# Key and value projections of a hybrid attention and DeltaNet layer, two blocks at a time by seven half products

## The chip, the core and the metric

The kernel runs on one core of a Trainium2 chip. The metric is the device time of one execution in microseconds; the median of three runs is shown, and the profile is of one further execution with its own time. TensorE (PE in the profile, its weight loads PEld) multiplies 128x128 weight tiles with streams of up to 512 columns into PSUM, which the kernel divides into six single banks of 512 float32 columns and one double one; VectorE (DVE), ScalarE (ACT) and GpSimd (POOL) work elementwise; SyncE (SP) issues the DMAs.

## The reference

A decoder layer on 512 tokens and 16 meta tokens ahead of them (528 in all), width 1024, eight heads in each of two branches that read the same normalised input:

```python
hn = rms_norm(h, norm_w)                      # 528 x 1024
proj = hn @ w_in                              # blocks aq ak av az dq dk dv dz db da ga gd
# attention: two softmax maps of 64 columns a head, p = p0 - lam * p1
o_a = rms_norm(diff_attention(aq, ak, av, lam), attn_norm_w) * 0.8
y_a = (o_a * silu(az)) @ w_branch_attn
# gated DeltaNet: causal convolution over 4 tokens and silu on dq, dk, dv; l2 norms;
# chunks of tokens: t_inv = inverse of (1 + strict lower part of beta * k k' * decay)
u, w = t_inv @ (v * beta), t_inv @ (k * beta * exp(gc))
v_new = u - w @ state;  o = q_dec @ state + a_intra @ v_new;  state = state * cd + k_dec' @ v_new
y_d = (rms_norm(o, dn_norm_w) * silu(dz)) @ w_branch_delta
merged = sigmoid(ga) * y_a + sigmoid(gd) * y_d
out = rms_norm(h + merged @ w_out, final_norm_w)[16:]
```

## The kernel before

**Products.** The normalised input stands transposed in SBUF as hn: eight blocks of 128 channels by 528 tokens, each as a high part (hnH, rounded to the engine's fast 32-bit type) and a low part (hnL, the rest). A weight block (128 output channels) is loaded as 128x1024 `raw`, and `split` makes a high part wh by a ScalarE cast and a low part wl by a VectorE subtraction. `product` then runs three passes (high by high, low by high, high by low: `PASSES`) over eight channel blocks: 24 matmuls of 512 columns for aq, az, dz, ga and gd, 48 matmuls of 272 and 256 columns for ak, av, dk and dv, 48 of 258 for dq. `dense` runs the blocks in the order of `dense_order`: four groups of two heads each, then gd; yd and ya (the two branch projections) and ga follow.

**The tail's seven products.** For yd and ya, `split_pair` and `pair_products` take two weight blocks at a time by a Winograd scheme: both blocks and the tokens are halved, and seven half products (`PRODUCTS`, p1 to p7) take the place of eight. Four weight tiles wa to wd are made of sums of weight halves, the input's sums (bt tiles) are made in `branch`, and the accumulator r is copied away between p1, p6 and p7 (`snap`) and added to others (`total`).

**Around the products.** dk, dv and dq go through `conv_silu` (ScalarE copies the PSUM banks into a row xp, then a scale, three VectorE steps, a tanh, and a product). `delta_pair` does the DeltaNet of two heads: key transposes and norms, k k' and k q' products, a mask E of decays, the 32x32 blocks sent through DRAM (scrm) into a layout in which VectorE solves them in 31 x 2 dependent steps (ts), back through DRAM (scrt, tds), the inverses TT, then four chunks of recurrent steps and the output into od. `attention` does one head into oa. The gates az and dz are written into oa and od first (`after_gate`), and od and oa of all eight heads (16 tiles of 256 KB) stay in SBUF until the tail.

**What sets the order.** Each piece is a generator that yields the engine, slot or event that it needs next. `Plan` runs them once ahead of time with a cost for each instruction (`Engine.time`), takes the task that can start first (ties by rank: splits 0, conv and gates 1, attention 2, dense 4) and so writes a fixed instruction order for each engine. Tiles with few copies are slots (`SLOTS`), PSUM banks are shared by kinds (`BANKS`: two each for pd, the dense products; pat; pdl). On the chip each engine runs its list in that order. SP issues all DMAs from one such list, weights ahead of use as the four raw tiles come free.

Of the kernel before, what the change touches and what calls it, by code (L numbers as in the profile page):

```python
# [24 lines left out]
H = 8  # L25
# [8 lines left out]
def dense_order():  # L34

    order = []
    for g in range(H // 2):
        for n in ("dk", "dv", "dq"):
            order += [(n, 2 * g), (n, 2 * g + 1)]
        order += [(n, 2 * g) for n in ("ak", "aq", "az", "av")]  # L40
        order += [("dz", 2 * g), ("dz", 2 * g + 1)]
        order += [(n, 2 * g + 1) for n in ("ak", "aq", "az", "av")]
    order += [("gd", c) for c in range(KB)]
    for p in range(KB // 2):
        order += [("yd", 2 * p), ("yd", 2 * p + 1), ("ga", p)]
    for p in range(KB // 2):
        order += [("ga", KB // 2 + p), ("ya", 2 * p), ("ya", 2 * p + 1)]
    return order
# [7 lines left out]

ORDER = dense_order()
PASSES = ((0, 0), (0, 1), (1, 0))


BANKS = dict(pd=2, pat=2, pdl=2)
# [6 lines left out]
SLOTS = dict(raw=4, w=2, wo=4, W=4, sn=5, st=1, tf=1, psc=1, xp=2, y=2, kT=2, qT=2, ktd=2, vr=2, E=2, eg=2, AT=2, MT=2, sc=2, km=1,  # L68
             ts=1, msub=1, TT=1, aq=2, ak=1, vT=1, vs=1, e=4, pT=2, pm=2, ao=1, th=8)
# [139 lines left out]
class Engine:  # L209
# [18 lines left out]
    def time(self, op, args, kw):  # L228
# [5 lines left out]
        if self.name == PE:  # L234
# [3 lines left out]
            if dt == F32:  # L238
                small = ins[0].shape[0] <= 64
                return 2 * max(2 * n / 2.4, 27 if small else 107)  # L240
            if dt == F32R:
                return n / 2.4 + 2.7 if n >= 256 else max(2 * n / 2.4, 107)
# [16 lines left out]
def hybrid_block(ctx: ExitStack, tc: tile.TileContext, x, meta, wblk, wbd, wout, pcol, prow, out):  # L259
    nc = tc.nc  # L260
    plan = Plan({**SLOTS, "wo": 0}, BANKS, ALL_BANKS)
# [43 lines left out]
    def tick(event, n):  # L305
        ticks[event] = ticks.get(event, 0) + 1
        if ticks[event] == n:
            done(event)

# [78 lines left out]
    def split(n, raw):  # L388

        yield ("w" if n < len(ORDER) or n - len(ORDER) in (4, 5) else "wo",)  # L390
        if n < len(ORDER) or n - len(ORDER) in (4, 5):
            wh, wl = (mk(wp, [P, D], F32R, t, SLOTS["w"]) for t in ("wh", "wl"))
        else:
            wo_slot[n] = plan.task.slot
# [7 lines left out]
        give("raw")  # L402
        done(f"w{n}")

    pairs, wos, wo_slot = {}, [], {}

    def split_pair(n, raws):

        (a1, a2), half = raws, (slice(0, D // 2), slice(D // 2, D))
        name = ORDER[n][0], ORDER[n][1] // 2  # L410
        pairs[name] = tiles = {}

        def parts_of(key, src, cols=slice(0, D)):
            yield ("W",)
            which = plan.task.slot
            wh, wl = Ws[which]
            yield ACT
            A.copy(out=wh[:, cols], in_=src)
# [3 lines left out]
            done(f"{key} {name}")  # L422

        yield "Ws"
        yield from parts_of("wa", a1)
        yield ("st",)
        st = mk(late["fp"], [P, D], F32, "st", 1)
        yield DVE
        V.tensor_tensor(out=st[:, half[0]], in0=a2[:, half[0]], in1=a2[:, half[1]], op=ALU.add)
        yield DVE  # L430
        V.tensor_tensor(out=st[:, half[1]], in0=st[:, half[0]], in1=a1[:, half[0]], op=ALU.subtract)
        yield from parts_of("wb", st)
        yield DVE
        V.tensor_tensor(out=a2[:, half[0]], in0=a1[:, half[0]], in1=a2[:, half[0]], op=ALU.subtract)
        yield from parts_of("wc", a2)
        give("raw")
        yield DVE
        V.tensor_tensor(out=a1[:, half[1]], in0=a1[:, half[1]], in1=st[:, half[1]], op=ALU.subtract)
        give("st")
        yield from parts_of("wd", a1[:, half[1]], half[0])  # L440
# [1531 lines left out]
```

## Time and profile before

| | us |
|---|---|
| median of three runs | 770.39 (769.94 to 771.57) |
| the profiled execution | 769.52 |
| its span in the trace | 767.8 |
| TensorE busy | 748.4 |
| VectorE busy | 551.3 |
| ScalarE busy | 477.6 |
| GpSimd busy | 73.1 |
| moved by DMA | 68.59 MB |

The trace names a line of code, but all instructions go through one helper (L224), so groups are told apart by their tiles: `bank<-hnH,wh` is a matmul of a weight tile wh with hnH into a PSUM bank, `wl<-raw,wh` the VectorE subtraction that makes a low part. A time with a count is that of the group. A matmul's duration overlaps with its neighbours', so the distance of starts tells what one costs.

### The profile page before, as it was taken

The numbers are of one execution on the slowest core, as the hardware profiler recorded it, in microseconds if no ns is written. First come the engines' busy times: TensorE is split into PE (matmuls) and PEld (weight loads), VectorE is DVE, ScalarE is ACT, GpSimd is POOL, SyncE is SP. The second block draws the span as 40 slices with busy tenths as digits, with TensorE's granted clock in tenths as the row PEclk, the third lists the DMA queues.
The fourth block names the chain that finished last, engine by engine and source line by source line (L and its number), as shares of the span: only waits on it lengthen the run. The fifth ranks groups of instructions, "written<-read, shape, count | busy, mean of one in ns | idle before, by whom it ended". The sixth has DMA issues, their size and how long they took to land.

```text
span 767.8 us, 14456 instructions
## 1 busy us (share of the span) xinstructions
PE 748.4 (97%) x5479; PEld 687.6 (90%) x5479; DVE 551.3 (72%) x1287; ACT 477.6 (62%) x1288; POOL 73.1 (10%) x101
## 2 busy tenths in 40 slices
PE   5999999999999999999999999999999999999996
PEld 4999887999989899988899998879888998899785
DVE  6778695577778668669757776964687868789553
ACT  5378478588556779756677865466775436455232
POOL 3121012011001212101201200000100000000001
PEclk9999999999999999999999999999999999999999
DMA  8142423011342201234311123231123323233702
GB/s 306 32 124 82 136 63 94 29 56 56 96 126 90 64 29 56 83 91 131 70 57 56 56 87 99 85 78 55 29 83 111 111 79 109 87 111 91 266 1 110
DMA packets 41974, 68.59 MB, mean 89 GB/s; under 512 B 20344, under 2 KB 25252, under 8 KB 41904
## 3 DMA queue, kind: packets, MB, share of 16 engines
q1 hardware_dynamic: 41904, 67.66, 28.1%
q8 instruction: 43, 0.70, 0.4%
q14 instruction: 27, 0.22, 0.1%
HBM read 64.44 MB, written 3.21 MB: 88 GB/s over the span
## 4 chain that ended last, share of the span: by engine, by line
PE 87%; DMA 4%; DVE 4%; ACT 3%; issue 1%; SPq 1%; POOL 0%; POOLq 0%; ACTq 0%; DVEq 0%
PE bank L224 84%; PE psc L224 3%; DMA scrt<-ts 1%; DMA tds<-scrt 1%; DMA xt<-in_x_dram 1%; DVE wl L224 1%; SPq L224 1%; DMA raw<-in_wout_dram 1%; ACT ak L224 1%; DVE xr L224 0%; ACT wh L224 0%; DVE hnL L224 0%; ACT TT L224 0%; DVE th L224 0%; DVE Wl L224 0%
## 5 line engine op out<-in xcount | busy, mean ns | idle before, releaser
L224 PE MATMUL bank<-hnH,wh 128*128 128x512 f32 (+3 forms) x944 | 317.1, 338 | 0.8 <-ACT hnH L224 0.8
L224 PE MATMUL bank<-hnH,wl 128*128 128x512 f32 (+3 forms) x944 | 301.4, 321 | 0.0
L224 PE MATMUL bank<-hnL,wh 128*128 128x512 f32 (+3 forms) x944 | 301.2, 321 | 0.0
L224 PEld LDWEIGHTS bank<-hnH,wh 128*128 128x128 f32 x944 | 177.1, 189 | 14.2 <-ACT hnH L224 1.0
L224 PEld LDWEIGHTS bank<-hnH,wl 128*128 128x128 f32 x944 | 176.9, 188 | 13.9
L224 PEld LDWEIGHTS bank<-hnL,wh 128*128 128x128 f32 x944 | 177.4, 189 | 10.3
L224 DVE TENSOR_TENSOR wl<-raw,wh 128x1024 fp32r<-128x1024 f32 x82 | 100.7, 1228 | 40.7 <-ACT wh L224 40.2
L224 ACT CAST wh<-raw 128x1024 fp32r<-128x1024 f32 x82 | 85.9, 1048 | 37.3 <-PE bank L224 32.5
L224 DVE SCALAR_TENSOR_TENSOR y<-xp,pc,y 128x528 f32<-128x528 f32 (+1 forms) x72 | 54.7, 760 | 2.2 <-ACT y L224 1.3
L224 ACT ACTIVATE e<-psc,ast 128x144 f32<-128x144 f32 (+3 forms) x64 | 34.6, 542 | 10.9 <-DVE ast L224 10.6
L224 PE MATMUL bank<-btH,Wh 128*128 128x256 f32 x128 | 36.0, 281 | 1.4 <-ACT sn L224 1.4
L224 PE MATMUL bank<-btH,Wl 128*128 128x256 f32 x128 | 35.7, 279 | 0.0
L224 PE MATMUL bank<-btL,Wh 128*128 128x256 f32 x128 | 35.7, 279 | 0.0
L224 ACT CAST Wh<-raw 128x1024 fp32r<-128x1024 f32 (+1 forms) x24 | 21.6, 906 | 19.8 <-PE bank L224 12.6
L224 DVE TENSOR_TENSOR ts<-ts,tmps 99x84 f32<-99x84 f32 (+23 forms) x124 | 28.2, 228 | 2.5
L224 DVE TENSOR_TENSOR tmps<-msub,ts 99x84 f32<-99x84 f32 (+23 forms) x124 | 27.7, 224 | 2.5
L224 ACT ACTIVATE sqk<-bank 128x128 f32<-128x128 f32 x64 | 17.9, 279 | 18.4 <-PE bank L224 17.6
L224 DVE TENSOR_REDUCE ast<-psc 128x1 f32<-128x528 f32 (+3 forms) x40 | 28.6, 714 | 0.5
L224 PE MATMUL psc<-ak,aq 128*128 128x264 f32 (+3 forms) x160 | 28.9, 302 | 0.0
L224 DVE TENSOR_TENSOR Wl<-raw,Wh 128x1024 fp32r<-128x1024 f32 (+1 forms) x24 | 24.9, 1043 | 4.9 <-ACT Wh L224 4.9
L224 PEld LDWEIGHTS bank<-btH,Wh 128*128 128x128 f32 x128 | 24.0, 187 | 2.2 <-ACT sn L224 1.9
L224 PEld LDWEIGHTS psc<-ak,aq 128*128 128x128 f32 x160 | 23.9, 189 | 1.5
(336 smaller groups left out, 1506.5 us busy)
## 6 DMA issues: line engine op xcount, KB each, us to landing
raw<-in_wblk_dram SPq DMA_DIRECT2D x96, 512.0 KB, 3.5
raw<-in_wout_dram SPq DMA_DIRECT2D x8, 512.0 KB, 3.9
xt<-in_x_dram SPq DMA_DIRECT2D x4, 512.0 KB, 7.6
E<-gcd SPq DMA_DIRECT2D x8, 256.0 KB, 5.2
xr<-in_x_dram SPq DMA_DIRECT2D x8, 256.0 KB, 7.0
out_dram<-xr SPq DMA_DIRECT2D x8, 256.0 KB, 2.3
msub<-scrm SPq DMA_DIRECT2D x12, 128.0 KB, 2.6
scrt<-ts SPq DMA_DIRECT2D x4, 136.1 KB
```

What stands on the lines that cost most here:

```text
L224: return real(*args, **kw)
```

## The change

Fourteen pairs of blocks go by the seven half products: (dk 2g, dk 2g+1) and (dv 2g, dv 2g+1) of the last three groups, and (ak h, av h) of all eight heads. The tokens are halved at 264. For that the kernel keeps the whole transposed input as well (`whole_`, in tiles `room`), makes four sums of it once (`ts_h`, `ts_l`), and makes the four weight sums of each pair. The pair's results are put together in xp or vT: three ScalarE copies and four VectorE sums out of PSUM. A fourth accumulator q takes p4.

To have room for this in SBUF, od and oa keep two heads each (`RING`, in room 0 and 2); the output of heads 0 to 5 of both goes to DRAM and comes back when the token sums are done with. The gate of head h waits until head h-2 is out. E, eg, TT and other tiles of a head pair share one buffer TM, and the solve's msub lies in room 1.

`products` of the DeltaNet now makes only k k' and no longer waits for the queries; k q' is made in `queries`. The order in a group is keys, values, ak av aq az of the even head (in the first group after the queries), queries, dz, ak av aq az of the odd head, dz. ga comes one place earlier. Weight tiles are one set of three for all blocks, and six in the tail. The costs in `Engine.time` for matmuls are raised.

```diff
-        order += [(n, 2 * g) for n in ("ak", "aq", "az", "av")]
...
+        k, v, q, z = ([(n, 2 * g), (n, 2 * g + 1)] for n in ("dk", "dv", "dq", "dz"))
+        a0, a1 = ([(n, 2 * g + i) for n in ("ak", "av", "aq", "az")] for i in range(2))
+        order += k + v + (a0 + q + z[:1] if g else q + z[:1] + a0) + a1 + z[1:]
+    order += [("gd", c) for c in range(KB)] + [("ga", 0)]
...
+PAIR_PRODUCTS = {**PRODUCTS, "p4": ("q", "wc", 1, "t4")}
+LAST = ("p2", "p5", "p4", "p3")
...
-BANKS = dict(pd=2, pat=2, pdl=2)
+BANKS = dict(pd=3, pat=2, pdl=2)
...
-SLOTS = dict(raw=4, w=2, wo=4, W=4, sn=5, st=1, tf=1, psc=1, xp=2, y=2, kT=2, qT=2, ktd=2, vr=2, E=2, eg=2, AT=2, MT=2, sc=2, km=1,
-             ts=1, msub=1, TT=1, aq=2, ak=1, vT=1, vs=1, e=4, pT=2, pm=2, ao=1, th=8)
+SLOTS = dict(raw=4, W=3, st=1, cn=1, wo=4, sn=5, tf=1, psc=1, xp=3, y=2, kT=2, qT=2, ktd=2, vr=2, TM=1, AT=2, MT=2, sc=2, km=1,
+             ts=1, aq=1, ak=1, vT=2, vs=1, e=4, pT=2, pm=2, ao=1, th=2)
+RING = dict(od=2, oa=2)
...
-                return n / 2.4 + 2.7 if n >= 256 else max(2 * n / 2.4, 107)
+                return n / 2.4 + (11 if n < 400 else 18) if n >= 256 else max(2 * n / 2.4, 107)
...
+        def sums():
+            yield ("st",)
+            yield DVE
+            V.tensor_tensor(out=st[:, h0], in0=a2[:, h0], in1=a2[:, h1], op=ALU.add)
+            yield DVE
+            V.tensor_tensor(out=st[:, h1], in0=st[:, h0], in1=a1[:, h0], op=ALU.subtract)
+            done(f"wb sum {name}")
+            yield DVE
+            V.tensor_tensor(out=a2[:, h0], in0=a1[:, h0], in1=a2[:, h0], op=ALU.subtract)
...
+        for key, src, cols in (("wa", a1, both), ("wb", st, both), ("wc", a2, both), ("wd", a1[:, h1], h0)):
+            if key != "wa":
+                yield f"{key} sum {name}"
+            yield ("W",)
+            which = plan.task.slot
+            yield ACT
+            A.copy(out=Ws[which][0][:, cols], in_=src)
+            spawn(low(key, src, cols, which))
...
+            def whole():
...
+                            A.copy(out=whole_[2 * (c // 4) + m][:, :, lo - HALF * m:hi - HALF * m],
+                                   in_=pt[:, c - dst[1].start:c - dst[1].start + 4, lo - t0:hi - t0])
+                if tick(bank_, 2):
+                    give("pat", pt)
...
+        for key, (x_, y_) in dict(t1=(1, 0), t3=(3, 1), t2=(3, 0), t4=(2, 3)).items():
+            yield DVE
+            V.tensor_tensor(out=whole_[of_sum[key]], in0=whole_[x_], in1=whole_[y_], op=ALU.subtract)
+            spawn(high_low(key))
...
+    def spill(t, h):
+        yield SP
+        S.dma_start(out=out_of[t, h], in_=gate[t][h])
...
         A.activation(out=th, in_=pd, func=AF.Tanh, scale=0.5)
+        if h >= RING[t]:
+            yield f"{t} out {h - RING[t]}"
+        yield DVE
+        V.scalar_tensor_tensor(out=gate[t][h], in0=th, scalar=1.0, in1=pd, op0=ALU.add, op1=ALU.mult)
...
+    def queries(i):
+        h = hs[i]
+        yield f"dq{h}"
+        yield f"m{h}"
...
+    def pair_of_blocks(n):
...
+        def total(m, tau, of, key, src=None):
+            yield f"{key} {n}"
+            yield from take(m)
+            yield DVE
+            dst = to[m][:, tokens[tau]]
+            V.tensor_tensor(out=dst, in0=acc[of], in1=dst if src is None else src, op=ALU.add)
...
+            if key == "p4":
+                spawn(total(1, 1, "t", "c", cn), -1)
+            if key == "p3":
+                yield f"c+ {n}"
...
+                for m, (a, b) in enumerate(PASSES):
+                    T.matmul(acc[bk], w[a][:, k * P:(k + 1) * P], x_[b], start=fresh and k == 0 and m == 0,
+                             stop=k == KB // 2 - 1 and m == 2, skip_group_check=not fresh)
...
+        for n in range(3):
+            Ws.append([mk(gp, [P, D], F32R, f"w{t}{len(Ws)}") for t in ("h", "l")])
+            plan.give("W", len(Ws) - 1)
```

## Rows read from the trace of the kernel before

**Rows 1.** The page: busy time of each engine, and the chain by engine.
```profile
PE 748.4 (97%) x5479; PEld 687.6 (90%) x5479; DVE 551.3 (72%) x1287; ACT 477.6 (62%) x1288; POOL 73.1 (10%) x101
...
PE 87%; DMA 4%; DVE 4%; ACT 3%; issue 1%; SPq 1%; POOL 0%; POOLq 0%; ACTq 0%; DVEq 0%
```

**Rows 2.** Busy time by stage: the start, then the four head pairs.
```profile
core 0: us, PE busy (x) PEld busy (x) DVE busy (x) ACT busy (x) POOL busy (x), PEclk, DMA share, GB/s
0.00:20.00 20.00, 10.71 (x65) 9.84 (x66) 12.58 (x29) 11.15 (x21) 7.55 (x19) 1.00 0.83 305
20.00:152.00 132.00, 130.70 (x1027) 120.81 (x1028) 95.58 (x266) 86.32 (x241) 17.03 (x23) 1.00 0.27 80
152.00:281.00 129.00, 128.96 (x1019) 120.60 (x1018) 93.18 (x237) 90.74 (x272) 15.70 (x20) 1.00 0.26 77
281.00:411.00 130.00, 130.00 (x1029) 121.73 (x1029) 94.50 (x239) 91.87 (x278) 16.45 (x20) 1.00 0.26 76
411.00:541.00 130.00, 129.32 (x1003) 119.87 (x1002) 92.12 (x235) 85.84 (x260) 9.96 (x13) 1.00 0.23 72
```

**Rows 3.** TensorE in order: start, duration; first and last of two runs.
```profile
164.27 0.29 PE L224 MATMUL bank<-hnH,wh 128*128 128x272 f32 x1
...
165.66 0.29 PE L224 MATMUL bank<-hnH,wl 128*128 128x272 f32 x1
...
167.73 0.28 PE L224 MATMUL bank<-hnH,wh 128*128 128x256 f32 x1
...
170.06 0.28 PE L224 MATMUL bank<-hnH,wl 128*128 128x256 f32 x1
```

**Rows 4.** VectorE groups by shape: count, busy us, mean ns, idle before.
```profile
L224 DVE TENSOR_TENSOR wl<-raw,wh 128x1024 fp32r<-128x1024 f32 x82 | 100.7, 1228 | 40.7 <-ACT wh L224 40.2
L224 DVE SCALAR_TENSOR_TENSOR y<-xp,pc,y 128x528 f32<-128x528 f32 x48 | 36.7, 765 | 1.3 <-ACT y L224 0.6
...
L224 DVE TENSOR_TENSOR sn<-bank,sn 128x256 f32<-128x256 f32 x24 | 10.0, 421 | 9.9 <-PE bank L224 8.9 <-ACT sn L224 0.9
...
L224 DVE SCALAR_TENSOR_TENSOR kT<-xp,y 128x528 f32<-128x528 f32 x8 | 5.6, 698 | 0.0
```

**Rows 5.** VectorE in order, in the tail: start, duration.
```profile
600.71 0.42 DVE L224 TENSOR_TENSOR sn<-bank,sn 128x256 f32<-128x256 f32 x1
601.04 0.68 DVE L224 TENSOR_TENSOR raw<-raw,raw 128x512 f32<-128x512 f32 x1
...
699.74 1.22 DVE L224 TENSOR_TENSOR Wl<-st,Wh 128x1024 fp32r<-128x1024 f32 x1
700.88 0.68 DVE L224 TENSOR_TENSOR od<-th,oa 128x512 fp32r<-128x512 f32 x1
701.48 0.69 DVE L224 TENSOR_TENSOR raw<-raw,raw 128x512 f32<-128x512 f32 x1
702.08 0.42 DVE L224 TENSOR_TENSOR sn<-bank,sn 128x256 f32<-128x256 f32 x1
```

**Rows 6.** Busy time in stretches of 20 us, columns as in rows 2.
```profile
160.00:180.00 20.00, 20.00 (x169) 19.77 (x169) 18.54 (x48) 17.10 (x63) 3.80 (x6) 1.00 0.24 80
...
640.00:660.00 20.00, 20.00 (x91) 16.36 (x90) 19.02 (x30) 10.97 (x15) 0.00 (x0) 1.00 0.33 106
...
680.00:700.00 20.00, 20.00 (x158) 19.15 (x157) 19.27 (x33) 10.92 (x17) 0.00 (x0) 1.00 0.38 117
700.00:720.00 20.00, 18.55 (x134) 17.28 (x133) 18.43 (x29) 11.00 (x17) 0.00 (x0) 1.00 0.59 187
```

**Rows 7.** ScalarE groups by shape, columns as in rows 4.
```profile
L224 ACT CAST wh<-raw 128x1024 fp32r<-128x1024 f32 x82 | 85.9, 1048 | 37.3 <-PE bank L224 32.5 <-DMA raw<-in_wout_dram 2.9 <-PE psc L224 0.8
...
L224 ACT COPY sn<-bank 128x256 f32<-128x256 f32 x24 | 8.9, 372 | 22.2 <-PE bank L224 22.1
...
L224 ACT CAST hnH<-bank 128x512 fp32r<-128x512 f32 x8 | 4.7, 588 | 3.4 <-PE bank L224 3.4
```

**Rows 8.** The tile od on VectorE: ns least, median, most; first to last start.
```profile
L224 DVE SCALAR_TENSOR_TENSOR od<-bank,wD,od x8: 746/751/752, 159.4 to 558.4; 128x512 f32<-128x512 f32 x8
```

**Rows 9.** DMA issues: size, median us to landing.
```profile
out_dram<-xr SPq DMA_DIRECT2D x8, 256.0 KB, 2.3
```

**Rows 10.** The chain in order of time: start, us, what.
```profile
708.27 4.14 DMA raw<-in_wout_dram
```

## What the change was predicted to do

> **What bounds the kernel now.** I read the page's busy shares and its chain first, then a table by stage, then single matmul starts. TensorE is busy for 97% of the span and carries 87% of the chain that ended last [rows 1]. The stage table cuts the span at the four head pairs (20 to 541 us): TensorE is busy for 130.70 of 132, 128.96 of 129, 130.00 of 130 and 129.32 of 130 us there, at granted clock 1.00, its upper level (2.4 GHz) [rows 2]. A busy TensorE need not be a full one, so the starts decide: in one key block twelve 272-column matmuls start within 1.39 us (11 steps of 0.1264 us), and twenty-one 256-column ones within 2.33 us (20 steps of 0.1165 us) [rows 3]. Nothing fits between them. The kernel is bound by matmul columns, and every matmul that goes is worth its step as long as its neighbours still arrive on time.
>
> VectorE is the one to watch. In the same four stages it is busy for 95.58, 93.18, 94.50 and 92.12 us, together 375.4 of 521 us (72%); ScalarE has 354.8 [rows 2].
>
> **The matmuls removed.** Two blocks cost 48 matmuls of 272 and 48 of 256 columns now: 48 x (0.1264 + 0.1165) = 11.66 us. The seven half products are 7 x 4 x 3 = 84 matmuls of 264 columns; a step of 264 lies between the two rows, 0.1215 us, so 10.20 us. One pair saves 1.46 us, fourteen save **20.4 us** [rows 3]. All of it lies on TensorE's path. No other matmul count changes: the query products are only parted from the key products, and the seven-product tail stays.
>
> The rows show a fixed part of some 10 to 13 ns per matmul beside its columns at 2.4 GHz. The Trainium skill, TensorE: Matmul & The Clock Gate, section Back-to-back issue gap, gives columns/2.4 plus 2.5 ns for a lone stream; by it 264 columns take 112.5 ns and the saving is 18.9 us. The trace does not agree, its steps are longer; the row is taken.
>
> **What VectorE gets.** Back to back, a 1024-column subtraction holds VectorE for 1.14 us and a 512-column one for 0.60; a 256-column sum out of PSUM holds it for 0.33 [rows 5] (their listed durations, 1.228 and 0.421 us, overlap the next start [rows 4]). Per pair: low halves 3 x 1.14 + 0.60 against 2 x 1.14 now, +1.74; four sums of weight halves, +2.40; four sums of 264 columns from PSUM where ScalarE copied before, 4 x 0.34 = +1.36. Together **5.5 us**, 77 us for fourteen. The four token sums add four subtractions and four low halves of 1056 columns, 8 x 1.17 = 9.4 us (1.14 scaled to the columns). VectorE's load in the four stages rises from 375.4 to 461.8 us, while TensorE's floor there falls from 521 to 500.6: a share of 92%. That is the crux. Three 20 us stretches already stand at 18.54, 19.02 and 19.27 us of VectorE with TensorE at 20.00 of 20 [rows 6]: such a share is possible without a hole in TensorE, but it is shown for 20 us, not for 500.
>
> **Holes that this opens.** First, inside a pair: the last product may start only when the partial sum of r has been copied (0.372 us [rows 7]) and added into the block (0.421 [rows 4]) after the matmul's own 0.28 [rows 3]; the product between covers 12 x 0.1215 = 1.46 us. Slack is some 0.4 to 0.5 us. If VectorE has just begun a 1.14 us operation, TensorE waits up to 0.64 us; averaged over where in it the sum arrives, 0.64 x 0.64 / 2 / 1.14 = 0.18. Fourteen pairs: 0 to 9 us, I take 2.5. Second, three weight tiles turn over: a freed tile needs one cast (1.048 [rows 7]), one subtraction (1.14) and hops, some 2.7 us, and the tightest is needed 36 matmuls = 4.4 us later. Queueing of more than 1.7 us stops TensorE; one operation ahead on each engine makes 2.2, so 0 to 0.5 us at two tiles a pair, 0 to 14 us, I take 1.5 since both queues must be unlucky at once. Third, the key and value pairs stand back to back: with their convolutions (three steps and a product, durations in [rows 4], some 2.7 us a block) they ask 2 x 13.1 = 26.2 us of VectorE for 20.4 us of matmuls. Splits, sums and the one convolution that frees the third xp row come to 18.3, so the rest can lag into the query and gate products, where a block asks VectorE for under 4 us per 5.6. 0 to 5.8 us in each of three groups, I take 1 each: 3.
>
> **What is moved, at nothing.** The inverses start without the queries, so the 62-step solve runs under keys, values and attention products; the single shared buffer TM keeps the next head pair's decays behind this pair's last step, and its end leaves some 10 us before they are needed. The gate products wait for the spill of the head two before: head 0's output is written at 159.4 us [rows 8], and in the new order its successor's gate comes some 50 us of matmuls behind the group's start at 152; a 256 KB write lands in 2.3 us [rows 9]. If that cover went, a gate would hold one of three PSUM banks and VectorE's queue behind its multiply. On SP a spill that waits holds the weight loads behind it; four raw tiles are two pairs, 20 us, of cover. The way back begins after the last value pair, with eight gate blocks (over 40 us of matmuls) ahead of its first reader. One tile for scaled queries instead of two: the next head's comes 31 us of matmuls or more later.
>
> **Start and end.** Twelve copies of the transposed input into whole_ lengthen the hold on two PSUM banks in the first 30 us; ScalarE is busy for only 11.15 of the first 20 us [rows 2]. 0 to 1.2 us (two copies of 0.588 [rows 7] on the way), I take 0.5. At the end the gate blocks (ga) come one place earlier, so the output weights may come earlier than now, where a 4.14 us load stands in the chain [rows 10] and TensorE lacks 1.45 of 20 us [rows 6]; against that a merged block now waits for its neighbour. Between -1.4 and +1.4, I take 0.
>
> **Sum.** Profiled execution 769.52 (span 767.8 and 1.7 around it) - 20.4 + 2.5 + 1.5 + 3 + 0.5 = 756.6. The median of the three runs is 0.9 above the profiled one: **757.5 us**, 1.7% less.
>
> **Rivals.** (a) VectorE becomes the bound of the four stages. Their length is then 461.8 us over the share s that it sustains. At 0.90 that is 513, 8 less than now: 763 us; at 0.89, 769. For it: the load above, and one solve of 62 dependent steps per group during which other work must wait its turn. Against it: rows 6, and attention's backlog that VectorE can always draw on. The Trainium skill, Perfetto Trace Analysis, section Identifying the Most-Contended Engine, would judge VectorE by occupancy and TensorE by its weight loads, not by matmul busy time. By that rule VectorE, at 92%, would bound the stages ahead of TensorE's weight loads (90% of the span [rows 1]), which is this rival; the starts in rows 3 speak against it for the kernel before. (b) Slower: the same mechanism below its point of balance, 461.8 / 521 = 0.886. At s = 0.86 the stages take 537 us, 16 more: 787 us. The kernel before never needed more than 0.73 in any of the four [rows 2], so no row excludes it. (c) Each pair loses in its own chain what it saves, both upper ends above together (0.64 + 1.0 us of 1.46): 770 us, no change. (d) All covers hold and TensorE stays full: 770.4 - 20.4 = 750 us.
>
> **Chances.** Forecast (751 to 762) 0.58, (d) 0.08, (a) 0.14, (c) 0.06, (b) 0.14. Range 750 to 771: it leaves out most of (b) and the outer edge of (d). A measurement of this kernel tells 0.2%, 1.5 us, from no change. Faster: 0.58 + 0.08 + 0.14 = 0.80; same 0.06; slower 0.14.
>
> **What will show it.** TensorE should lose 168 matmuls and start its 264-column ones about 0.1215 us apart. If the forecast holds, its idle time in the four stages is 4 to 10 us, in pieces under 1 us that end on a sum (VectorE) or a low half, and the stages last some 508 us with VectorE at 0.90 to 0.92. If (a) or (b), the pieces are longer, end on VectorE throughout, and lie in the key and value pairs; if (c), they recur in every pair at the same product. The tail from the first branch product should last as before within 2 us. The prediction is wrong if VectorE's own load is more than 5.5 us a pair, if a gate waits for a spill, or if the way back from DRAM is late for the branch products.

## The result, and the profile after

The changed kernel takes 763.90 us in the median of fifteen executions (760.91 to 768.06), the kernel before 770.54: a ratio of 0.9906, 95% interval 0.9886 to 0.9925. That is 6.6 us less; 13 were forecast. The range of 750 to 771 holds it, the forecast's own 751 to 762 does not. One further execution of the changed kernel (3139 us) and one of the run e6_before_new_costs (2616 us) were slow as a whole and are not counted. The profiled execution is one of the longer ones, 767.75 us with a span of 766.0; a second profiled execution (762.45 us, span 760.7, the run a1_again) stands beside it below.

The page after, busy time of each engine and the chain by engine, answers [rows 1]:

```profile
PE 740.0 (97%) x5311; PEld 671.6 (88%) x5311; DVE 620.2 (81%) x1427; ACT 500.4 (65%) x1318; POOL 89.6 (12%) x102
...
PE 74%; DVE 10%; ACT 10%; issue 2%; DMA 1%; POOL 1%; SPq 0%; POOLq 0%; DVEq 0%; ACTq 0%
```

TensorE has exactly 168 matmuls less (5479 to 5311), but it carries 74% of the chain where it carried 87%: VectorE and ScalarE now stand in it with 10% each. Being "97% busy" before and after hides this. The stages, cut as in [rows 2]:

```profile
core 0: us, PE busy (x) PEld busy (x) DVE busy (x) ACT busy (x) POOL busy (x), PEclk, DMA share, GB/s
0.00:20.00 20.00, 8.69 (x50) 8.03 (x51) 12.89 (x26) 13.56 (x27) 8.71 (x20) 1.00 0.80 308
20.00:152.00 132.00, 128.72 (x991) 117.19 (x990) 114.76 (x294) 87.55 (x222) 25.01 (x21) 1.00 0.25 75
152.00:281.00 129.00, 127.37 (x957) 116.93 (x957) 110.30 (x273) 92.68 (x274) 15.83 (x20) 0.96 0.27 85
281.00:411.00 130.00, 129.32 (x1016) 119.80 (x1015) 113.29 (x280) 99.49 (x293) 19.49 (x20) 1.00 0.27 84
411.00:541.00 130.00, 129.32 (x983) 117.67 (x982) 108.08 (x276) 97.34 (x291) 14.05 (x15) 1.00 0.33 105
```

VectorE has 446.4 of 521 us (86%), 71.0 more than before; TensorE stands for 6.3 us in the four stages, where it stood for 2.0; and in the second stage the granted clock is 0.96, where it was 1.00 throughout. TensorE within one half product (start, duration; the first and the ninth of nine):

```profile
427.11 0.28 PE L231 MATMUL bank<-sumH,wh 128*128 128x264 f32 x1
...
428.08 0.28 PE L231 MATMUL bank<-sumH,wl 128*128 128x264 f32 x1
```

Eight steps take 0.97 us, 0.1213 each, against 0.1215 priced. The Trainium skill, TensorE: Matmul & The Clock Gate, section Back-to-back issue gap, has columns/2.4 plus 2.5 ns for an isolated matmul, by which it would be 112.5 ns; this trace does not agree with it, 264 columns at 2.4 GHz and 11 ns more fit.

What TensorE waited for (total us, times, longest; the first nine of fourteen rows):

```profile
PE bank L231 <- ACT st L231: 7.5, 1, 7.5
PE bank L231 <- ACT sn L231: 2.1, 1, 2.1
PE bank L231 <- DVE ss L231: 1.5, 1, 1.5
PE bank L231 <- DVE qT L231: 1.3, 3, 0.9
PE bank L231 <- DVE TM L231: 1.3, 3, 0.5
PE bank L231 <- ACT hnH L231: 1.3, 1, 1.3
PE bank L231 <- ACT pmT L231: 1.2, 1, 1.2
PE bank L231 <- ACT room L231: 0.9, 1, 0.9
PE bank L231 <- DVE sumL L231: 0.4, 1, 0.4
```

The first, third and sixth are the start; before, the same view has 7.3, 1.2 and 0.8 us for them. `pmT` (attention) and `sn` (the tail) have grown from 0.7 and 1.4 us. New are `room` (the second copy of the input holds a PSUM bank at the start) and `qT`, the scaled queries of the DeltaNet. `TM` stands where the kernel before had `td` and `t`, 1.2 us together. No wait ends on a weight tile (wh, wl), and none on a spilled gate. The longest wait for `qT` ends at 79.87 us. VectorE's list ahead of it (start, duration):

```profile
77.75 1.20 DVE L231 TENSOR_TENSOR wl<-raw,wh 128x1024 fp32r<-128x1024 f32 x1
78.88 0.33 DVE L231 SCALAR_TENSOR_TENSOR MT<-bank,sc,TM 128x128 f32<-128x128 f32 x1
79.15 0.67 DVE L231 SCALAR_TENSOR_TENSOR qT<-xp,y 128x512 f32<-128x512 f32 x1
```

So the short step stands behind a low half and a step of the DeltaNet, in a stretch in which VectorE has no room left. VectorE's 86% is an average of unequal stretches of 20 us, two of which are (columns as in the stages above):

```profile
60.00:80.00 20.00, 18.45 (x129) 16.27 (x128) 19.90 (x32) 16.72 (x40) 6.56 (x6) 1.00 0.03 5
300.00:320.00 20.00, 20.00 (x164) 19.56 (x163) 19.96 (x43) 19.50 (x59) 7.33 (x8) 1.00 0.47 156
```

VectorE is full in both. TensorE loses 1.55 us in the first, which has the waits for `qT`, and nothing in the second.

**The clock.** TensorE around 266 us, in the profiled execution; in brackets the idle time before, and what ended it:

```profile
265.55 0.28 PE L231 MATMUL bank<-hnH,wl 128*128 128x264 f32 x1
266.99 0.33 PE L231 MATMUL bank<-vm,pmT 96*128 96x128 f32 x1 [1.16 <-ACT pmT L231]
...
268.01 0.41 PE L231 MATMUL bank<-hnL,wh 128*128 128x264 f32 x1
268.22 0.42 PE L231 MATMUL bank<-hnH,wl 128*128 128x264 f32 x1
```

After 64 products of 32x32 (264.2 to 265.2), three matmuls and 1.16 us of waiting, the step of a 264-column matmul is 0.21 us instead of 0.12: the granted clock has fallen to its lower level, 1.2 GHz, and it stays there for 10 us. These 20 us in this execution (columns as in the stages above):

```profile
260.00:280.00 20.00, 18.84 (x159) 16.88 (x159) 11.20 (x23) 10.84 (x27) 0.27 (x1) 0.74 0.15 54
```

and in the second one, a1_again:

```profile
260.00:280.00 20.00, 18.81 (x198) 17.32 (x197) 12.72 (x28) 15.07 (x42) 1.01 (x1) 1.00 0.16 54
```

Clock 0.74 against 1.00, with the same instructions in the same order and the same wait ahead (1.16 us in both). In the profiled execution the clock falls once more, behind the tail's wait described below (0.91 over 700 to 720 us). So the clock falls in some executions and not in others, and the executions differ by it: at a mean clock of 0.996 to 0.998 they take 760.9 to 762.6 us, at 0.989 to 0.992 765.2 to 768.1. The kernel before takes 768.4 to 773.5 us in its executions, with medians between 769.4 and 770.9, and it too is slower where the mean clock is lower (769.4 at 0.998, 773.1 at 0.991).

**The tail.** The chain near 705 us (start, us, what), answering [rows 10]:

```profile
703.99 4.93 DMA raw<-in_wout_dram
708.92 0.02 issue
708.95 1.04 ACT wh L231
709.99 0.28 ACT sn L231
710.27 0.04 issue
710.32 1.80 PE bank L231 x12
```

ScalarE's list has the cast of the fifth output weight block ahead of the copy `sn` of a partial sum. The block's load is late, the cast waits for it, the copy waits behind the cast, and TensorE waits 2.1 us (3.0 in the second execution) for a copy of 0.28 us that had nothing to do with the load.

### The profile page after: what moved, and what is told of

Same layout as the page of the kernel before. It is cut to its first block, busy times and chain, and to the rows that moved or that the text cites. A ratio compares the mean times of both kernels' runs of the same rounds, so it can differ in the third digit from the quotient of the medians.

```text
span 766.0 us, 14381 instructions
## 1 busy us (share of the span) xinstructions
PE 740.0 (97%) x5311; PEld 671.6 (88%) x5311; DVE 620.2 (81%) x1427; ACT 500.4 (65%) x1318; POOL 89.6 (12%) x102
## 4 chain that ended last, share of the span: by engine, by line
PE 74%; DVE 10%; ACT 10%; issue 2%; DMA 1%; POOL 1%; SPq 0%; POOLq 0%; DVEq 0%; ACTq 0%
PE bank L231 71%; PE psc L231 3%; ACT wh L231 2%; DVE wl L231 2%; DVE y L231 1%; ACT TM L231 1%; DMA xt<-in_x_dram 1%; POOL km L231 1%; ACT ak L231 1%; ACT e L231 1%; DMA raw<-in_wout_dram 1%; ACT ktd L231 1%; DVE ak L231 1%; DVE ast L231 1%; ACT y L231 1%
## 5 line engine op out<-in xcount | busy, mean ns | idle before, releaser
L231 PE MATMUL bank<-hnH,wh 128*128 128x512 f32 (+4 forms) x664 | 233.6, 355 | 1.6 <-ACT hnH L231 1.3
L231 PE MATMUL bank<-hnL,wh 128*128 128x512 f32 (+4 forms) x664 | 222.0, 337 | 0.0
L231 PE MATMUL bank<-hnH,wl 128*128 128x512 f32 (+4 forms) x664 | 221.7, 337 | 0.0
L231 DVE TENSOR_TENSOR wl<-raw,wh 128x1024 fp32r<-128x1024 f32 (+1 forms) x120 | 134.4, 1121 | 20.2 <-ACT wh L231 19.6
L231 ACT CAST wh<-raw 128x1024 fp32r<-128x1024 f32 (+1 forms) x120 | 116.4, 970 | 48.6 <-PE bank L231 34.5
L231 PEld LDWEIGHTS bank<-hnH,wl 128*128 128x128 f32 x664 | 124.3, 189 | 14.0
L231 PEld LDWEIGHTS bank<-hnL,wh 128*128 128x128 f32 x664 | 124.5, 189 | 9.5
L231 PE MATMUL bank<-sumH,wh 128*128 128x264 f32 x224 | 68.0, 303 | 0.0
L231 PE MATMUL bank<-sumL,wh 128*128 128x264 f32 x224 | 63.9, 285 | 0.4 <-DVE sumL L231 0.4
L231 PE MATMUL bank<-sumH,wl 128*128 128x264 f32 x224 | 63.8, 285 | 0.0
L231 ACT ACTIVATE e<-psc,ast 128x144 f32<-128x144 f32 (+3 forms) x64 | 34.7, 542 | 18.4 <-DVE ast L231 16.6
```

The source lines that it names most:

```text
L231: return real(*args, **kw)
```

## Experiments

**The changed kernel once more** (a1_again), unaltered.

> The changed kernel unaltered, for a second profile of the same program and for the granted clock of each execution. Theory (the clock falls to its lower level in a thin stretch of TensorE in some executions and not in others): times between 761 and 768, longer where the mean granted clock is lower, some 5 us between 0.998 and 0.989, and the falls of the second profile not all where those of the first stand. Rival (the spread is of the chip, not of the clock): time and mean clock don't go together.

Measured: 763.51 us (762.18 to 766.50), ratio 0.9919 [0.9891, 0.9946]. The time is longer where the mean clock is lower (762.45 at 0.997, 766.50 at 0.991), as the theory has it. The profiled execution, span 760.7 at a mean clock of 0.997, has no fall of the clock before its end, and the same holes.

### Is it VectorE's amount?

**Four weight sums left out** in all fourteen pairs (e1_sums_out): `sums` only passes the events on, so the products of wb, wc and wd are made with weights that are not summed.

```diff
+            if n in PAIRED:
+                done(f"wb sum {name}")
+                done(f"wc sum {name}")
+                yield f"wa {name}"
+                done(f"wd sum {name}")
+                return
...
-        for key, src, cols in (("wa", a1, both), ("wb", st, both), ("wc", a2, both), ("wd", a1[:, h1], h0)):
+        for key, src, cols in (("wa", a1, both), ("wb", a2 if n in PAIRED else st, both), ("wc", a2, both), ("wd", a1[:, h1], h0)):
```

> Leaves out the four sums of weight halves of the fourteen pairs (raw halves are split and multiplied instead), 14 x 2.4 = 34 us of VectorE; TensorE and ScalarE do what they did. Theory (the holes in TensorE come from VectorE's load): the holes of the four stages, some 8 to 10 us more than in the kernel before, fall to under 4 us, and with them the falls of the clock: 753 to 757 us. Rival (the holes come from the new order and from the chains through DRAM): 760 to 764 us as before this edit.

Measured: 760.75 us (759.07 to 762.07), ratio 0.9871 [0.9843, 0.9899]. VectorE's busy time falls from 619.9 to 591.0 us, the time by 2.8. This is the rival: TensorE's idle time in the four stages does not fall (6.7 us, where the changed kernel has 6.3), and nine tenths of what was taken from VectorE came to nothing. At 86% VectorE's whole amount is not the bound. That it is none in single full stretches isn't shown: over 60 to 80 us VectorE still has 19.25 of 20 us in this run, and TensorE 18.76.

**Sums on GpSimd** (e2_sums_pool): `yield POOL` and `G.tensor_tensor` for the same four sums.

```diff
+            eng, X = (POOL, G) if n in PAIRED else (DVE, V)
-            yield DVE
-            V.tensor_tensor(out=st[:, h0], in0=a2[:, h0], in1=a2[:, h1], op=ALU.add)
+            yield eng
+            X.tensor_tensor(out=st[:, h0], in0=a2[:, h0], in1=a2[:, h1], op=ALU.add)
...
```

> Moves the four sums of weight halves of the fourteen pairs from VectorE to GpSimd, which is busy for 12% of the span. Theory (VectorE's load): as the sums left out, 753 to 758 us, if GpSimd makes a sum of 512 columns in about 1.2 us or less. Rival (the two engines hinder each other, or weight tiles come too late): no gain, 761 us or more, with waits of ScalarE for the sums.

Measured: 800.03 us, ratio 1.0393 [1.0339, 1.0448]: the rival, and 36 us slower than a1_again. VectorE has 56 operations less and is busy for 627.8 us, more than in a1_again. Groups of this run (count, busy us, mean ns, idle before):

```profile
L231 DVE SCALAR_TENSOR_TENSOR y<-xp,pc,y 128x528 f32<-128x528 f32 x48 | 42.5, 892 | 0.6 <-ACT y L231 0.4
L231 DVE TENSOR_TENSOR vT<-bank,vT 128x264 f32<-128x264 f32 x16 | 6.7, 421 | 0.0
L231 POOL TENSOR_TENSOR st<-st,raw 128x512 f32<-128x512 f32 x14 | 22.9, 1634 | 1.1
```

and two of the changed kernel:

```profile
L231 DVE SCALAR_TENSOR_TENSOR y<-xp,pc,y 128x528 f32<-128x528 f32 x48 | 36.3, 764 | 0.1
L231 DVE TENSOR_TENSOR vT<-bank,vT 128x264 f32<-128x264 f32 x16 | 6.8, 425 | 0.2
```

A sum takes GpSimd 1.3 to 1.6 us where VectorE needs 0.6. In the same run VectorE's operations with both tensors in SBUF are slower in the mean (y 764 to 892 ns), those with one in PSUM are not (425 to 421). The mean hides two kinds: the 8 of the 48 steps y that overlap such a sum take 1.59 us, the other 40 take 0.75; of the 16 sums vT four overlap one too, and take 0.42 us like the rest. The Trainium skill, SBUF — State Buffer, section SBUF: two separate sides, states this: a VectorE operation with two SBUF inputs and a GpSimd operation that reads SBUF exclude each other. The trace agrees.

**Two of the sums three times** (e3_sums_thrice), 56 operations more.

```diff
+            for _ in range(3 if n in PAIRED else 1):
+                yield DVE
+                V.tensor_tensor(out=st[:, h0], in0=a2[:, h0], in1=a2[:, h1], op=ALU.add)
```

(and the same for the second sum)

> Makes two of the four sums of each pair three times, the same result each time: 14 x 2.4 = 34 us more of VectorE, nothing else. Theory (VectorE is close to its limit in the four stages): its share there rises from 86% to 92% or so, the holes grow by 10 us or more: 772 to 785 us. Rival (VectorE has room, the holes have another cause): under 767 us.

Measured: 809.79 us, ratio 1.0533 [1.0472, 1.0594], well above the 772 to 785 of the theory: 46 us more for 34.7 us of VectorE (619.9 to 654.6). Its longest new waits of TensorE:

```profile
PE bank L231 <- DVE kT L231: 6.8, 2, 4.0
PE bank L231 <- DVE vT L231: 5.1, 3, 3.5
PE bank L231 <- DVE e L231: 5.0, 3, 2.6
```

They end on VectorE and last up to 4.0 us, and the mean clock of the execution is 0.976: on 806.6 us that is 0.024 x 806.6 = 19 us of missing clock (an estimate), where a1_again misses 0.003 x 760.7 = 2. VectorE's share from 20 to 541 us is 456.4 of 521, 88%. So VectorE does become a bound, as rivals (a) and (b) have it, somewhere between the changed kernel and one with 34.7 us more: 28.9 us less give 2.8, 34.7 us more cost 46. The repeated sums also stand between a block's load and its weight tiles; how much of the 46 us is this delay is not separated, but none of this run's waits of TensorE ends on a weight tile.

### Which pairs pay?

**Eight pairs** (e4_ak_only), keys and values of attention only.

```diff
-PAIRS = [n for n, (name, i) in enumerate(ORDER) if name == "ak" or name in ("dk", "dv") and i > 1 and i % 2 == 0]
+PAIRS = [n for n, (name, i) in enumerate(ORDER) if name == "ak"]
```

> Of the fourteen pairs only the eight (ak, av) go by seven products; the six (dk, dk) and (dv, dv) go by eight as before, so TensorE gets 72 matmuls more (6 x 1.46 = 8.8 us) and VectorE some 33 us less. Theory A: the 13 us of holes that the change added belong to fixed things (start, token sums, single chains, tail) and to TensorE's own dense order, not to the key and value pairs; then 763.5 + 8.8 less 1 to 2 = 770 to 772, no gain left over the kernel before. Theory B: the key and value pairs, standing back to back, make most of the holes in the four stages (some 6 us) and set off the clock's falls (3 us); then 762 to 767.

Measured: 763.94 us (763.67 to 764.33), ratio 0.9916 [0.9896, 0.9937]. The same as with fourteen pairs: the 72 matmuls of the other six, 8.75 us, are worth nothing in the median. Theory B in time; what its reason is worth, the next runs tell. Its second stage:

```profile
152.00:281.00 129.00, 129.00 (x1019) 119.85 (x1018) 104.31 (x268) 96.72 (x300) 14.71 (x20) 1.00 0.27 85
```

and the second stage with fourteen pairs, in a1_again:

```profile
152.00:281.00 129.00, 127.34 (x996) 117.43 (x996) 112.36 (x278) 96.60 (x288) 15.81 (x20) 1.00 0.27 85
```

Without the key and value pairs TensorE is full in this stage, and all four executions have a mean clock of 0.998 or 0.999. With fourteen the best execution is 760.91, with eight 763.67: at full clock the six pairs give 2.8 us, of 8.75.

**Eleven pairs** (e10_dv_only): the (dv, dv) pairs too, so that no pair of keys stands directly ahead of one of values. In the last three groups the pair of values still stands directly ahead of the first (ak, av).

```diff
+PAIRS = [n for n, (name, i) in enumerate(ORDER) if name == "ak" or name == "dv" and i > 1 and i % 2 == 0]
```

> Eleven pairs: the eight (ak, av) and the three (dv, dv); the three (dk, dk) go by eight products, 36 matmuls more than in the changed kernel (4.4 us), VectorE 16 us less. With eight pairs the time was the same as with fourteen: six pairs saved 8.75 us of matmuls and brought as much in holes. Theory A: the holes come where two pairs with their convolutions follow each other at once, and with blocks of eight products between the pairs most of the saving is kept: 759 to 761.5. Theory B: each pair beyond the eight brings its own holes, whatever stands beside it; 763 to 765 like both.

Measured: 765.75 us (765.42 to 767.50), ratio 0.9956 [0.9939, 0.9972]. Just above theory B's 763 to 765: three pairs more are 2 us slower than eight, although two pairs with convolutions no longer follow each other at once. That the (ak, av) pair follows the values at once stays as a possible cause.

**No pairs** (e11_no_pairs): everything else of the change. The old copies for attention's keys and values (`in_two`) come back; the token sums are made and not used.

```diff
+PAIRS = []
...
+                if (name, i) == ("av", 7):
+                    done("sums free")
```

> Everything of the change but the pairs: new order, early inverses, spilled gates, the second copy of the input, the token sums (made, not used), three weight tiles and six in the tail, the new costs; keys and values go by eight products as before, so TensorE has the 5479 matmuls of the kernel before (20.4 us more than the changed kernel) and VectorE some 77 us less. With it the four points are 0, 8, 11 and 14 pairs. Theory A: what is moved costs nothing but the start (1.5 us) and the tail's longer hole (1.5 us), and the pairs' own holes are what ate the rest; 771 to 774, so that eight pairs brought 7 to 10 us and the last six nothing. Theory B: what is moved costs 5 us or more by itself (gates behind spills, chains in another place), and pairs keep nearly all they save; 775 to 784. Theory C: the moved parts gain by themselves; below 769.

Measured: 776.29 us (776.22 to 776.55), ratio 1.0078 [1.0050, 1.0107]. With the same 5479 matmuls as before, 6.6 us slower than the kernel before beside it (769.69): in theory B's range, although the pairs do not keep nearly all that they save, as it says. Four of its waits of TensorE:

```profile
PE bank L231 <- DVE qT L231: 1.9, 2, 1.0
PE bank L231 <- DVE ss L231: 1.4, 1, 1.4
PE bank L231 <- ACT hnH L231: 1.3, 1, 1.3
PE bank L231 <- POOL vm L231: 1.2, 1, 1.2
...
```

The products with the queries (`qT`) wait on VectorE although its share is 74% (383.9 of 521 us). In full stretches again: the two waits end at 234 and 366 us, and over 200 to 220 and 340 to 360 us VectorE has 18.75 and 19.30 of 20 us. The points, with what TensorE's starts say: the surplus is the time from the first to the last matmul's start in the profiled execution, less the sum of the steps, each priced at the median step of its shape over these five traces.

| pairs | matmuls | median us | surplus us |
|---|---|---|---|
| kernel before | 5479 | 769.4 to 770.9 | 17.1 |
| 0 | 5479 | 776.29 | 23.9 |
| 8 | 5383 | 763.94 | 24.1 |
| 11 | 5347 | 765.75 | 32.0 |
| 14 (a1_again) | 5311 | 763.51 | 31.6 |

The change without its pairs adds 6.8 us of surplus, eight pairs add almost none and bring the 11.7 us of their matmuls, six more add 7.5 of the 8.75 that they save. Of these 7.5, 1.8 lie in the tail: TensorE's wait for `sn` is 1.2 us with eight pairs and 3.0 in a1_again. And each row has an order of its own that the planner wrote; as the order alone can move the time by more than 10 us (next section), the rows don't show how much of a difference is the pairs' and how much the new order's.

### The planner's cost, the clock, and two repairs

**The old cost of matmuls** in the changed kernel (e5_old_costs), and **the new one in the kernel before** (e6_before_new_costs); nothing else differs but the order that the planner writes.

```diff
-                return n / 2.4 + (11 if n < 400 else 18) if n >= 256 else max(2 * n / 2.4, 107)
+                return n / 2.4 + 2.7 if n >= 256 else max(2 * n / 2.4, 107)
```

> The changed kernel with the planner's old cost for the fast 32-bit matmuls (columns / 2.4 + 2.7 ns). Nothing else differs but the order that comes out of it. Theory A: the order hardly depends on it; 762 to 766, within 0.3% of the changed kernel. Theory B: the new costs, which are nearer to the measured steps, keep the planned order true on the chip (work of the other engines planned 8 to 15 ns per matmul too late or too early), and without them holes grow by some us in every stage; 768 to 776.

Measured: 774.79 us (774.69 to 775.52), ratio 1.0060 [1.0043, 1.0078]: theory B. TensorE stands for 13.8 us in the four stages; the longest new waits of TensorE are

```profile
PE bank L231 <- DVE qT L231: 4.0, 1, 4.0
PE bank L231 <- DVE vT L231: 2.8, 1, 2.8
```

and the mean clock is 0.987 to 0.993.

In the kernel before, the second experiment is the reverse of that diff, with the cost of plain 32-bit matmuls raised as in the change:

```diff
-                return 2 * max(2 * n / 2.4, 27 if small else 107)
+                return 2 * max(2 * n / 2.4 + 4, 32 if small else 107)
...
-                return n / 2.4 + 2.7 if n >= 256 else max(2 * n / 2.4, 107)
+                return n / 2.4 + (11 if n < 400 else 18) if n >= 256 else max(2 * n / 2.4, 107)
```

> The kernel before with the changed kernel's cost of matmuls in the planner, nothing else; all 5479 matmuls stay. Theory A: the new costs pay where VectorE is near its limit (the changed kernel lost 11 us with the old ones); the kernel before has 72% of VectorE and 5 us of holes in its stages, so there is little to gain: 767 to 771. Theory B: the order gains by itself, and part of what looked like the gain of the seven products is the planner's: 757 to 765.

Measured: 781.19 us (780.67 to 781.68, three executions), ratio 1.0151 [1.0134, 1.0168]; where in the kernel the 12 us go is not shown. Both theories miss: the kernel before loses 12 us with the new figures, the changed kernel 11 us with the old ones. The new figures are the nearer to the measured steps (0.1213 us here, 0.1264 at 272 columns in [rows 3]), yet they help one kernel and harm the other. Compared under one cost line the change would be a loss of 0.6% (old figures) or a gain of 2.2% (new).

**TensorE kept busy ahead of thin products** (e7_fill): 32 unused matmuls, outside the planner, so that the order stays.

```diff
+    def fill(b, n):
+        for _ in range(n):
+            nc.tensor.matmul(b[:, 256:512], hn[0][:, 0, 0:P], hn[0][:, 0, 0:256], start=True, stop=True)
...
+        fill(px, 4)
...
+            px = bank("pdl")
+            fill(px, 1)
...
```

> The changed kernel, same planned order, with 32 matmuls of 256 columns more (3.7 us if all lay on the path; the results are not used): four ahead of the 32x32 products of the inverse in each of the four groups, and one ahead of each set of 64x64 products, where TensorE would else stand or run small matmuls. Theory A: the clock falls in the changed kernel's slower executions (267 us in one, 147 and 270 in another of a variant) come from these thin stretches, and the added matmuls lie partly in waits; the mean granted clock is 0.996 or more in every execution, all times lie within 2 us, median 762 to 764.5. Theory B: the falls have another cause; the clock spreads from 0.989 to 0.998 as before and the median rises by the full price to 766 to 768.

Measured: 764.51 us, five executions within 764.17 to 764.76 at mean clocks of 0.996 to 0.999; ratio 0.9934 [0.9920, 0.9947]. Over 260 to 280 us of the profiled one the granted clock is 1.00. The spread of 7 us is gone, which speaks for theory A; its price is 3.3 us over the best executions of the changed kernel, nearly the full 3.7, so the time gained at the median is paid back. Five executions make the link likely; they don't show how the chip decides.

**Two raw tiles for one weight tile in the tail** (e8_tail_raw).

```diff
-        for n in range(3):
+        for n in range(2):
             Ws.append([mk(gp, [P, D], F32R, f"w{t}{len(Ws)}") for t in ("h", "l")])
             plan.give("W", len(Ws) - 1)
+        for n in range(2):
+            raws.append(mk(gp, [P, D], F32, f"raw{len(raws)}"))
+            plan.give("raw", len(raws) - 1)
```

> In the tail five weight tiles and six raw tiles take the place of six and four, so that the fifth and sixth output weight block can be loaded before the first is split. Theory A: the hole near 708 us of the span (2.3 us in the first profile, 3.0 in the second) is ScalarE's queue: the cast of the fifth output block waits for its load, and behind it stands the copy of a partial sum that TensorE waits for. With the load 10 us earlier the hole goes, and the fall of the clock that followed it in one profile: 2.3 to 3.5 us less, 760 to 761.5. Theory B: the copy is late for another reason, or the sixth weight tile was needed: the hole stays or turns up at another product, 763 to 766.

Measured: 762.17 us (eight of ten executions within 762.03 to 762.33, two at 766.56 and 771.33), ratio 0.9906 [0.9878, 0.9934]. TensorE's wait for `sn` falls to 0.5 us, as theory A has it, but two others come, on weight tiles:

```profile
PE bank L231 <- ACT wh L231: 1.0, 1, 1.0
PE bank L231 <- DVE wl L231: 0.5, 1, 0.5
```

The sixth tile was needed, as theory B has it, and the time lies between the two theories' ranges; the best execution is 1.1 us slower than that of the changed kernel. The profiled execution is the one of 771.33: its clock is 0.83 over 140 to 160 and 0.77 over 260 to 290 us, again at the inverses.

**The second copy of the input by GpSimd** (e9_whole_pool), from hnH and hnL instead of out of PSUM.

```diff
-                            yield ACT
-                            A.copy(out=whole_[2 * (c // 4) + m][:, :, lo - HALF * m:hi - HALF * m],
-                                   in_=pt[:, c - dst[1].start:c - dst[1].start + 4, lo - t0:hi - t0])
+                            yield POOL
+                            G.tensor_tensor(out=whole_[2 * (c // 4) + m][:, :, lo - HALF * m:hi - HALF * m],
+                                            in0=hn[0][:, c:c + 4, lo:hi].bitcast(F32),
+                                            in1=hn[1][:, c:c + 4, lo:hi].bitcast(F32), op=ALU.add)
...
```

> The second copy of the transposed input (whole_) is no longer made by ScalarE out of PSUM at the start, but by GpSimd as the sum of the high and the low part, after both. Theory A: the start lost 1.5 us because these copies held the PSUM banks and ScalarE's queue; it comes back, 761.5 to 762.5, and TensorE is busy 10.5 or more of the first 20 us. Theory B: GpSimd's sums slow VectorE's low parts in the same 20 to 30 us, as its sums of weights slowed VectorE over the whole span (800 us), and the token sums come later: 764 to 768.

Measured: 762.45 us (760.88 to 765.80), ratio 0.9904 [0.9874, 0.9934]. The first 20 us of this run:

```profile
0.00:20.00 20.00, 10.08 (x61) 9.37 (x62) 12.86 (x26) 11.79 (x21) 10.72 (x22) 1.00 0.85 307
```

and its second longest wait of TensorE:

```profile
PE bank L231 <- DVE sumL L231: 2.7, 1, 2.7
```

TensorE works 1.4 us more in the first 20 us (10.08, where theory A asked for 10.5), and waits 2.3 us longer at the first pair, for the token sums. The time is theory A's, the reason why nothing is gained is theory B's; the best execution stays at 760.88. No variant beats the changed kernel by more than the intervals.

## Why the prediction came out as it did

Half of the forecast gain came. The range held because it was wide enough to take in rival (a); the forecast itself was 6.4 us too low, and none of its three signs of being wrong came (a heavier VectorE, a gate behind a spill, a late way back). Put together from the runs: 770.5 + 6.6 (the change without pairs) - 12.4 (eight pairs) - 8.75 + 6.0 (six pairs, and what they lose in the best executions) + 3 (median against best) = 765, against 763.9 measured. These terms are differences of the same medians and best executions, so that they add up proves nothing; they show where the time went. Against the prediction's own terms:

- **Matmuls removed, -20.4:** right, in count and in step.
- **VectorE, 5.5 us a pair and 9.4 for the token sums:** over the whole span 60.4 us between no pairs and fourteen (559.8 to 620.2), 4.3 a pair; the token sums and what goes with them 8.5 (551.3 to 559.8). The share became 86%, not 92%. Single operations were priced right (a 1024-column low half 1.22 us, a 264-column sum 0.425, as in [rows 4]); the four weight sums alone are 2.1 us a pair (28.9 us for fourteen in e1_sums_out) where 2.40 were priced, and which of the other two items is too high, the runs don't tell.
- **Hole inside a pair, 2.5:** the visible waits of a last product are 0.24, 0.17 and 0.38 us over all fourteen pairs, 0.8. The slack of 0.4 us held nearly always.
- **Weight tiles, 1.5:** none in the four stages.
- **Key and value pairs, 3:** mis-sized. They lose 6.0 of 8.75 us in the best executions, some 1.8 of it in the tail, and the reason given, two pairs with their convolutions in direct succession, does not explain it: with eleven pairs there is no such succession, and the loss stays. The waits end mostly on steps of the DeltaNet and attention chains, on VectorE, ScalarE or GpSimd, hardly in the pairs. That the pairs' work stands ahead of these steps in an engine's list is likely (the `qT` step above stands behind a low half), but wasn't tested by moving a step.
- **What is moved, at nothing; start 0.5:** this is the step that failed. The change without its pairs cost 6.6 us, for the moved parts, the raised costs and the new order together. The spills and the way back were indeed free, and no wait ends on them. The start took 1.5 to 2. In the stages the waits of size are those of the queries' products for VectorE (`qT`, 1.9) and one on GpSimd (`vm`, 1.2); the rest ends in no listed wait. The raised costs stood in the diff and had no term in the sum at all, though they alone move either kernel by 11 to 12 us. How much of the 6.6 is each moved part's is open, as they weren't undone one by one; the costs and the order don't add up (with the new costs in both, the other moved parts gain 4.9: 781.2 to 776.3).
- **The end, 0:** from its first matmul with btH to the end of the span the tail lasts 176.3 us where it was 173.4, and 175.5 in the second execution; "within 2 us" was narrowly missed. The new wait is ScalarE's queue behind a late load.
- **The clock:** not in the sum; 0 to 7 us in an execution. The median lies 3.0 us above the best execution, where the kernel before, measured beside it, has 1.0.

Of the rivals, (a) gives a time (763 to 769) that fits, by a mechanism that does not: at 86%, VectorE's whole amount is not what sets the time, though it is full in single stretches. The share that rivals (a) and (b) turn on, 0.886 at the point of balance, was near the mark: with the sums made three times VectorE sustained 0.88, and 46 us were lost. (b) lies that one step of load away, (d) did not come; (c)'s outcome, a pair that loses what it saves, came for the last six pairs in the median, but not at its place, a product inside the pair. The expected signs were half right: idle time of 6.3 us (4 to 10 forecast) in pieces of at most 1.16 us, but hardly any ends on a sum or a low half, and VectorE stands at 0.86, not 0.90 to 0.92.

## What to carry to other kernels

Saving matmuls pays in full only while the other engines' chains still meet their times: here eight replacements gave all they promised and the next six a third of it, or nothing in the median. Price each group of replacements apart, and look for short steps that wait in an engine's list behind long work, or behind a cast whose load is late. Look at an engine's share in short stretches: an average of 86% hides stretches with over 99%. And where a planner writes the order, treat every change of its costs as a change of its own, and run it alone: here it weighed as much as some ninety matmuls.

## What the runs showed that was not expected

- With an unchanged list of instructions the granted clock fell to 1.2 GHz in some executions after the inverses' thin products and a 1.2 us wait, for 10 us, and not in others; with 32 matmuls more in those places the mean clock was 0.996 or more in five of five.
- Beside GpSimd's sums of two SBUF tensors (1.3 to 1.6 us) VectorE's step with two SBUF inputs took 1.59 us instead of 0.75, 17% more in the mean of all; sums that read PSUM stayed as they were.
- The planner's raised costs of matmuls (8 and 15 ns for a fast 32-bit one; in the kernel before those of the plain 32-bit ones as well) moved the kernel before by +12 us and the changed one by -11.
